# The first feed-forward's second product by seven products for eight, with its weight sums made in DRAM beside its first product

## The chip, the cores and the metric

One core of one Trainium2 chip runs the whole program. The metric is device time in microseconds of one execution, the median of several. A run's profile covers one execution of its own.

## The reference

Two layers over 512 tokens of width 1024. Each layer is a gated feed-forward (ffn1), a token mixer with three kinds of attention, and a second gated feed-forward (ffn2), each followed by a residual and a layer norm. All of it is float32. What the change touches is the second matrix of the first feed-forward of layer 0.

```python
def _swiglu(x, w1, w2):
    gt, up = jnp.split(x @ w1, 2, axis=-1)
    return (jax.nn.silu(gt) * up) @ w2          # w1: 1024 x 5632, w2: 2816 x 1024

for l in range(DEPTH):                          # DEPTH = 2
    x = _layer_norm(DN_ALPHA * x + 0.5 * _swiglu(x, ffn1_w1[l], ffn1_w2[l]), ln1_g[l], ln1_b[l])
    mix = _token_mix(x, w_in[l], ...)
    x = _layer_norm(DN_ALPHA * x + mix, ln2_g[l], ln2_b[l])
    x = _layer_norm(DN_ALPHA * x + 0.5 * _swiglu(x, ffn2_w1[l], ffn2_w2[l]), ln3_g[l], ln3_b[l])
```

## The kernel before

**Arithmetic.** Every float32 operand is split into a high part (ScalarE copies it to fp32r) and a low part (VectorE subtracts), and a product of two operands is three matmuls: high by high, low by high, high by low. `wsplit` (L155 ScalarE, L156 VectorE) does that for weights, `parts` (L483) for activations.

**A feed-forward** (`ffn`) has two products on TensorE, one after the other. The first makes the hidden rows, 22 blocks `f` of 128. The blocks 0 to 3 are plain; from block 4 on, `seven` loads the block's gate columns (`rg`, L422) and up columns (`ru`, L423), makes sums of them on VectorE (`ws`, L429 to L432), splits them, and `strassen` does seven products for eight, 84 matmuls with 256 columns. In it ScalarE copies the first two products out of PSUM (`sn`, L525), and TensorE's sixth product, which writes the same bank again, waits for that copy. `evac` (`t`, L473, then L474) writes the finished hidden block into `ha` or `hb`.

The second product contracts the 22 chunks of the hidden rows with w2. There are two forms of it. `rows_ln` is plain: for each chunk 4 token blocks by 2 column halves by 3, 24 matmuls of 128x512. `strassen_rows` takes the first 18 chunks as 9 pairs, each pair by seven products for eight, which is 42 matmuls for 48, and the last 4 chunks (`NTAIL`) plain. It needs four sums of the pair's blocks of w2, called t1 to t4. They do not depend on any activation.

**The weight sums.** `weight_sums` puts a queue of steps into `sums`; each step is one DMA from GpSimd's queue (L397) of 128x3x512 float32, 768 KB, from DRAM to DRAM, for three pairs at once. A step either copies a block of w2 into `ts` or adds a block to what stands there. `sums_step` issues the next step: a one-column copy on GpSimd first waits for a tile that some engine has just written, and so paces the steps. In the kernel before, the steps run in the mixer, for the two feed-forwards that come behind it. The first feed-forward of layer 0 has no mixer ahead of it, gets `ts = None`, and so takes `rows_ln`.

**Order.** TensorE and GpSimd run in the order of the code. VectorE, ScalarE and SyncE's DMA queue run in the order that a scheduler chose from its own estimate of times when the program was built; on the chip each of them keeps that order. Tiles come from rings of buffers: the raw weight columns `raw` have three. In the built program the gate columns of block f+1 go, from block 6 on, into the buffer that held the gate columns of block f.

**Side traffic.** In the first product of layer 0, `seven` also issues one table broadcast per block from GpSimd (`bvec`, L435 and L436), 16 in all, behind the block's `ws`.

Of the kernel before, what the change touches and what calls it, by code (L numbers as in the profile page):

```python
# [9 lines left out]
F32 = mybir.dt.float32  # L10
F32R = mybir.dt.float32r
BF = mybir.dt.bfloat16
AF = mybir.ActivationFunctionType
OP = mybir.AluOpType
# [50 lines left out]
def body(tc, a, out, depth=DEPTH):  # L65
# [199 lines left out]

    def strassen_rows(w2, ts, sp, plain, ln, clear, nxt, tmp):


        def acc8():
            return [ps(name="acc") for _ in range(8)]  # L270
# [12 lines left out]
        for p in range(NS):  # L283
            if p == 2:
                extra.pool = rp
            rb, ra = wraw(), wraw()
            nc.sync.dma_start(flat(rb)[:, 0:512], w2[2 * p * P:(2 * p + 1) * P, 0:512])
            nc.sync.dma_start(flat(rb)[:, 512:1024], ts[:, p, 1024:1536])
            nc.sync.dma_start(flat(ra), ts[:, p, 0:1024])
            sh, sl = sp(p)  # L290
            ub, ua = wsplit(rb), wsplit(ra)
            prods = [(0, 0, ub, lo4), (1, 3, ub, hi4), (2, 1, ua, hi4), (3, 2, ua, lo4)]
            for i, j, w, c in prods[:1] + prods[2:] + prods[1:2] if p == 0 else prods:
                for b in range(2):
                    mm(a1[2 * i + b], (sh[:, j], sl[:, j]), w, b, c, p == 0, p == NS - 1)
# [34 lines left out]
        for p in range(NS):  # L330
            uc, d, dc = weights(p)
            sh, sl = sp(p, True)
            prods = [(0, 1, uc, lo4), (1, 0, uc, hi4), (2, 2, d, dc)]
            for i, j, w, c in prods[2:] + prods[:2] if p == NS - 1 else prods:
                for b in range(2):
                    mm(a2[2 * i + b], (sh[:, j], sl[:, j]), w, b, c, p == 0, False)
            if p in (1, 2):
                merge(p - 1)
        rest = []
        for k in range(2 * NS, KF):  # L340
            rest.append((k, plain(k), wrows(w2, k)))
        extra.pool.release()
        extra.pool = None
# [34 lines left out]
        return pts  # L378

    NTAIL = 4  # L380
    NS = 9
    NG = 3
    sums = deque()

    def weight_sums(w2):


        ts = dram.tile([P, NS, 2048], F32, name="ts", tag="ts", bufs=3)
        n = NS // NG

        def step(g, i):
            c = slice(n * g, n * g + n)
            v = w2[2 * n * g * P:2 * n * (g + 1) * P].rearrange("(q two p) f -> two p q f", two=2, p=P)
            b11, b12, b21, b22 = (v[j][:, :, 512 * k:512 * k + 512] for j in range(2) for k in range(2))
            t1, t3, t2, t4 = (ts[:, c, 512 * k:512 * k + 512] for k in range(4))
            o, x = ((t1, b11), (t3, b12), (t2, b22), (t1, b12), (t4, b21), (t3, b22), (t2, t1), (t4, t2))[i]
            nc.gpsimd.dma_start(o, x, **({"accum_op": OP.add} if i in (3, 5, 6, 7) else {}))  # L397

        for g in range(NG):
            sums.extend(lambda g=g, i=i: step(g, i) for i in range(8))  # L400
        return ts

    def sums_step(t, psum=False):
# [59 lines left out]
    def ffn(l, w1, w2, which, xap, xa, wts, pend, done_prev, last, nxt, ts):  # L463
# [9 lines left out]
            nc.scalar.activation(t, pg, AF.Silu)  # L473
            nc.vector.tensor_tensor(hpart(f), t, pu, op=OP.mult)  # L474

        made, hs = {}, {}

        def h_parts(k, t):
            parts(t[:, 0], t[:, 1], hpart(k))
            hs[k] = t  # L480

        def parts(hi, lo, x):
            nc.scalar.activation(hi, x, AF.Copy)  # L483
            nc.vector.tensor_tensor(lo, x, hi.bitcast(F32), op=OP.subtract)
# [67 lines left out]
        evac(0, pts[0], pts[1])  # L552
        evac(1, pts[2], pts[3])
        for f in range(2, KF):
            if f == KF - 1 and ts is None:
                for k, n in enumerate(("hi", "lo")):
                    h_parts(k, wt.tile([P, KD, P], F32R, name=n, tag=n, bufs=3)
                            .rearrange("p (a b) c -> p a (b c)", a=2))
            elif f == KF - 1:
                w = [wt.tile([P, KD, P], F32R, name=n, tag=n, bufs=3).rearrange("p (a b) c -> p a (b c)", a=4)  # L560
                     for n in ("hi", "lo")]
                v, sn = (st.w1p.tile([P, 2, 256], F32, name=n, tag=n, bufs=2) for n in ("v", "sn"))
                made[0] = s_parts(0, w, v, sn[:, 0])
# [14 lines left out]
        for tb in range(NB):  # L578
            nc.gpsimd.dma_start(xa[tb], x_sp[tb * P:(tb + 1) * P, :])
        hsp = pool("hsp", side="right", reuse_waits="tile")  # L580
        ln = LN(hsp, which, l, xa, 0.5, last, ts is not None)

        def wload(k):
            if k not in hs:
                h_parts(k, hsp.tile([P, 2, S], F32R, name="hs", tag="hs", bufs=6))
            return wrows(w2, k)

        def pair():
            return [hsp.tile([P, 4, 256], F32R, name=n, tag=n, bufs=4) for n in ("sh", "sl")]
# [20 lines left out]
            r = [ln.row(n) for n in "GB"]  # L610
            return [[t[:, 0:S] for t in v]] + [[t[:, 0:S], t[:, S:D]] for t in r]

        if ts is None:
            wts, pend = rows_ln(KF, wload, lambda k: hs[k][:, 0], lambda k: hs[k][:, 1], ln, NA, fa.release, nxt)
        else:
            wts, pend = strassen_rows(w2, ts, sp, plain, ln, fa.release, nxt, tmp)

        def done():
            nx_close()
# [903 lines left out]
        tables(*tabs)  # L1523
        init.release()
    wts = pre
    ts = [None]
    for l in range(depth):
        fin = l == depth - 1
        wts, pend, done, xap, xa = ffn(l, a["ffn1_w1"][l], a["ffn1_w2"][l], 0, xap, xa, wts, pend, done, False,
                                       lambda: mix_first(l), ts.pop(0))  # L1530
        ts += [weight_sums(w) for w in [a["ffn2_w2"][l]] + ([] if fin else [a["ffn1_w2"][l + 1]])]
        wts, pend, done, xap, xa = mix(l, wts, pend, done, xap, xa, lambda: ffn_first(a["ffn2_w1"][l]))
        assert not sums
        wts, pend, done, xap, xa = ffn(l, a["ffn2_w1"][l], a["ffn2_w2"][l], 2, xap, xa, wts, pend, done, fin,
# [31 lines left out]
```

## Time and profile before

| what | us |
|---|---|
| median of 3 runs (2469.45 to 2471.69) | 2469.77 |
| the profiled execution: its own time | 2472.68 |
| the profiled execution: its span | 2470.9 |
| TensorE busy, of the span | 2443.8 (99%) |
| VectorE busy | 1763.6 (71%) |
| ScalarE busy | 1171.5 (47%) |
| GpSimd busy | 328.0 (13%) |

The granted TensorE clock is 0.997 over the span. In the profile's rows PE is a matmul, PEld a weight load, DVE VectorE, ACT ScalarE, POOL GpSimd, and SPq SyncE's DMA queue. A row of the timeline begins with the start and the duration in us. Matmuls overlap in the pipeline, so the rate at which they go is the distance from one start to the next, not the duration of one. A DMA row's duration is that of the issue; the time to its landing stands in the view of its line.

### The profile page before, as it was taken

Reading aid. Unit: us, or ns where it says so; the run is one execution under the profiler, and the core shown is the slowest. Engines: PE = TensorE matmul, PEld = TensorE weight load, DVE = VectorE, ACT = ScalarE, POOL = GpSimd, SP = SyncE. Lnnn points to the kernel's source line nnn. Section 1 sums busy time; section 2 is a strip of 40 time slices with the busy share of each in tenths; the row PEclk is TensorE's granted clock in tenths of the full one; section 3 lists DMA queues with packets and bytes.
Section 4 is the critical chain, followed back from the end, with each engine's and each line's share of the span. In section 5 each row is a group of like instructions: output and inputs, shape, how many; then the busy total and the mean of one; then the engine's idle time right before and its main releaser. Section 6 shows DMA issues by size and latency. Waiting matters only on the chain. (4 is left out here: it accounts for less than half of the span.)

```text
span 2470.9 us, 41023 instructions
## 1 busy us (share of the span) xinstructions
PE 2443.8 (99%) x15529; PEld 2157.1 (87%) x15529; DVE 1763.6 (71%) x3554; ACT 1171.5 (47%) x2262; POOL 328.0 (13%) x598
## 2 busy tenths in 40 slices
PE   9999999999999999999999999999999999999998
PEld 8999888788888789999889998877888888899987
DVE  7888355687653367988879889756776543698887
ACT  4444334576632343445534446445766422344463
POOL 2000000144432210000000000001444100000000
PEclk9999999999999999999999999999999999999999
DMA  7345434656579952336633346646655833323463
GB/s 207 104 120 143 140 96 127 183 152 146 127 209 237 251 172 82 103 104 210 203 98 99 104 144 211 186 113 168 157 155 114 227 102 122 112 87 109 131 210 127
DMA packets 411462, 364.07 MB, mean 147 GB/s; under 512 B 19720, under 2 KB 351640, under 8 KB 411264
## 3 DMA queue, kind: packets, MB, share of 16 engines
q1 hardware_dynamic: 381968, 279.92, 38.5%
q0 software_dynamic: 29296, 81.53, 13.2%
q8 instruction: 122, 2.00, 0.3%
q14 instruction: 76, 0.62, 0.1%
HBM read 334.07 MB, written 74.51 MB: 165 GB/s over the span
## 5 line engine op out<-in xcount | busy, mean ns | idle before, releaser
L156 DVE TENSOR_TENSOR lo<-raw,hi 128x1024 fp32r<-128x1024 f32 (+2 forms) x384 | 450.5, 1182 | 384.4 <-ACT hi L155 380.0
L155 ACT ACTIVATE hi<-raw 128x1024 fp32r<-128x1024 f32 (+2 forms) x384 | 390.1, 1023 | 598.5 <-DMA raw<-in_ffn_w_dram 136.3
L176 PE MATMUL pj<-xh,hi 128*128 128x512 f32 (+1 forms) x720 | 267.0, 371 | 0.1
L177 PE MATMUL pj<-xl,hi 128*128 128x512 f32 (+1 forms) x720 | 254.7, 354 | 1.1 <-DVE xl L242 1.1
L178 PE MATMUL pj<-xh,lo 128*128 128x512 f32 (+1 forms) x720 | 254.7, 354 | 0.0
L518 PE MATMUL pg<-xh,hi 128*128 128x256 f32 x864 | 245.0, 284 | 1.6 <-ACT sn L525 1.6
L518 PE MATMUL pg<-xh,lo 128*128 128x256 f32 x864 | 244.5, 283 | 0.0
L518 PE MATMUL pg<-xl,hi 128*128 128x256 f32 x864 | 244.5, 283 | 0.0
L438 ACT ACTIVATE hi<-ws 128x1024 fp32r<-128x1024 f32 x144 | 151.2, 1055 | 159.7 <-DVE ws L430 69.9
L439 DVE TENSOR_TENSOR lo<-ws,hi 128x1024 fp32r<-128x1024 f32 x144 | 175.4, 1221 | 17.8 <-ACT hi L438 17.7
L275 PE MATMUL acc<-hi,sh 128*128 128x512 f32 x450 | 175.4, 390 | 0.0
L275 PE MATMUL acc<-lo,sh 128*128 128x512 f32 x450 | 175.1, 389 | 0.0
L275 PE MATMUL acc<-hi,sl 128*128 128x512 f32 x450 | 175.1, 389 | 0.0
L518 PEld LDWEIGHTS pg<-xh,hi 128*128 128x128 f32 x864 | 165.8, 192 | 2.7 <-ACT sn L525 2.5
L518 PEld LDWEIGHTS pg<-xl,hi 128*128 128x128 f32 x864 | 165.8, 192 | 0.2
L518 PEld LDWEIGHTS pg<-xh,lo 128*128 128x128 f32 x864 | 165.8, 192 | 0.0
L518 PE MATMUL pu<-th,hi 128*128 128x256 f32 x576 | 163.0, 283 | 0.0
L518 PE MATMUL pu<-tl,hi 128*128 128x256 f32 x576 | 163.0, 283 | 0.0
L518 PE MATMUL pu<-th,lo 128*128 128x256 f32 x576 | 163.0, 283 | 0.0
L178 PEld LDWEIGHTS pj<-xh,lo 128*128 128x128 f32 x720 | 136.3, 189 | 19.6
L176 PEld LDWEIGHTS pj<-xh,hi 128*128 128x128 f32 x720 | 136.7, 190 | 15.3 <-issue 3.1
L177 PEld LDWEIGHTS pj<-xl,hi 128*128 128x128 f32 x720 | 137.0, 190 | 13.0 <-DVE xl L242 1.6
(368 smaller groups left out, 6259.9 us busy)
## 6 DMA issues: line engine op xcount, KB each, us to landing
raw<-in_ffn_w_dram SPq DMA_DIRECT2D x237, 512.0 KB, 4.0
ts<-in_ffn_w_dram POOLq DMA_DIRECT2D x54, 768.0 KB, 9.1
raw<-in_w_in_dram SPq DMA_DIRECT2D x56, 512.0 KB, 4.1
raw<-in_w_gate_dram SPq DMA_DIRECT2D x48, 512.0 KB, 5.2
raw<-ts SPq DMA_DIRECT2D x39, 512.0 KB, 4.2
ts<-ts POOLq DMA_DIRECT2D x18, 768.0 KB, 9.5
x_sp<-xa POOLq DMA_DIRECT2D x24, 512.0 KB, 6.1
ks<-hl SPq DMA_DIRECT2D x96, 128.0 KB, 2.4
```

What stands on the lines that cost most here:

```text
L155: nc.scalar.activation(hi[:, c], raw[:, c], AF.Copy)
L156: nc.vector.tensor_tensor(lo[:, c], raw[:, c], hi[:, c].bitcast(F32), op=OP.subtract)
L176: nc.tensor.matmul(o, hi[:, k], vh, start=first, stop=False)
L177: nc.tensor.matmul(o, hi[:, k], vl, start=False, stop=False)
L178: nc.tensor.matmul(o, lo[:, k], vh, start=False, stop=last)
L275: nc.tensor.matmul(o, xx[:, t], ww[:, c], start=first and i == 0, stop=last and i == 2)
L438: nc.scalar.activation(hi, x, AF.Copy)
L439: tt(lo, x, hi.bitcast(F32), op=OP.subtract)
L518: nc.tensor.matmul(o, wx, vx, start=first and k == 0 and i == 0, stop=k == 3 and i == 2, skip_group_check=True)
```

## The change

The first feed-forward of layer 0 gets weight sums for 6 pairs (chunks 0 to 11) and takes `strassen_rows` too. Chunks 12 to 17 are done plainly in the same accumulators, chunks 18 to 21 as before. Its 16 steps (two groups of three pairs, eight steps each) are issued as follows: twelve in the first product, at blocks 4 to 20 except each third, each paced by the hidden block before; four beside the pairs 0 to 3 of the second product, paced by the pair's split hidden rows. The order of the steps changes for all feed-forwards: t1, t3, t2 copied and then added to, for all groups, and t4 (a copy and an add) of all groups at the end. `rows_ln` stays in use for the mixer's output alone.

```diff
 def strassen_rows(w2, ts, sp, plain, ln, clear, nxt, tmp):
+        NS = ts.shape[1]
...
             sh, sl = sp(p)
+            sums_step(sh[:, 0].bitcast(F32))
             ub, ua = wsplit(rb), wsplit(ra)
...
+        for k in range(2 * NS, KF - NTAIL):
+            x, w = plain(k), wrows(w2, k)
+            for tb in range(NB):
+                for hf in range(2):
+                    mm(accs[tb][hf], x, w, tb, slice(4 * hf, 4 * hf + 4), tb >= 2 and hf == 1 and k == 2 * NS, False)
         rest = []
-        for k in range(2 * NS, KF):
+        for k in range(KF - NTAIL, KF):
...
-    def weight_sums(w2):
+    def weight_sums(w2, ns):
...
-            o, x = ((t1, b11), (t3, b12), (t2, b22), (t1, b12), (t4, b21), (t3, b22), (t2, t1), (t4, t2))[i]
-            nc.gpsimd.dma_start(o, x, **({"accum_op": OP.add} if i in (3, 5, 6, 7) else {}))
-
-        for g in range(NG):
-            sums.extend(lambda g=g, i=i: step(g, i) for i in range(8))
+            o, x = ((t1, b11), (t3, b12), (t2, b22), (t1, b12), (t3, b22), (t2, t1), (t4, b21), (t4, t2))[i]
+            nc.gpsimd.dma_start(o, x, **({"accum_op": OP.add} if i in (3, 4, 5, 7) else {}))
+
+        for r in (range(6), range(6, 8)):
+            for g in range(ns // n):
+                sums.extend(lambda g=g, i=i: step(g, i) for i in r)
...
         for f in range(2, KF):
-            if f == KF - 1 and ts is None:
...
+            if f >= 4 and f % 3:
+                sums_step(hpart(f - 1))
...
-    ts = [None]
+    ts = [weight_sums(a["ffn1_w2"][0], 6)]
...
-        ts += [weight_sums(w) for w in [a["ffn2_w2"][l]] + ([] if fin else [a["ffn1_w2"][l + 1]])]
+        ts += [weight_sums(w, 9) for w in [a["ffn2_w2"][l]] + ([] if fin else [a["ffn1_w2"][l + 1]])]
```

The scheduler made another order of the first product too. Three places of it are shown. The numbers in the names are the program's own: in the kernel before, `raw_1891`, `raw_2144` and `raw_2269` belong to the blocks 14, 16 and 17, and `pg_1919` and `pg_2045` to the blocks 14 and 15; in the kernel after, `raw_1908`/`raw_1909`, `raw_2034`/`raw_2035` and `raw_2162` are the blocks 14, 15 and 16, and `pg_1936` and `pg_2062` the blocks 14 and 15.

ScalarE around the copy `sn` of block 15, before:

```order
L155 ACTIVATE hi_2273<-raw_2269 128x1024
L473 ACTIVATE t_2014<-pg_1919 128x512
L525 ACTIVATE sn_2072<-pg_2045 128x512
L438 ACTIVATE hi_2279<-ws_2284 128x1024
L440 ACTIVATE dh_2155<-raw_2144 128x512
L438 ACTIVATE hi_2277<-ws_2283 128x1024
```

and after:

```order
L155 ACTIVATE hi_2166<-raw_2162 128x1024
L444 ACTIVATE hi_2042<-ws_2048 128x1024
L446 ACTIVATE dh_2046<-raw_2035 128x512
L444 ACTIVATE hi_2044<-ws_2049 128x1024
L479 ACTIVATE t_2031<-pg_1936 128x512
L527 ACTIVATE sn_2089<-pg_2062 128x512
```

Ahead of `sn` of block 15 stood the split of the gate columns of block 17, two blocks on; now the last such split ahead of it is that of block 16, one block on.

VectorE at the sums of block 14, before (`raw_1892` are the up columns of block 14, `pu_1668` belongs to block 12):

```order
L156 TENSOR_TENSOR lo_1896<-raw_1891,hi_1895 128x1024
L474 TENSOR_TENSOR ha_473<-t_1636,ha_473 128x512
L429 TENSOR_TENSOR ws_1905<-raw_1892 128x512
L431 TENSOR_TENSOR ws_1906<-raw_1891,raw_1892 128x512
L430 TENSOR_TENSOR ws_1905<-ws_1905,raw_1891 128x512
L432 TENSOR_TENSOR ws_1906<-raw_1891,ws_1905 128x512
L529 TENSOR_TENSOR v_1720<-pu_1668,sn_1694 128x256
L530 TENSOR_TENSOR v_1720<-pu_1668,v_1720 128x256
```

and after (`pu_1809` belongs to block 13):

```order
L156 TENSOR_TENSOR lo_1913<-raw_1908,hi_1912 128x1024
L435 TENSOR_TENSOR ws_1922<-raw_1909 128x512
L447 TENSOR_TENSOR dl_1793<-raw_1781,dh_1792 128x512
L539 TENSOR_TENSOR pg_1680<-pg_1680,v_1733 128x256
L436 TENSOR_TENSOR ws_1922<-ws_1922,raw_1908 128x512
L480 TENSOR_TENSOR ha_474<-t_1775,ha_474 128x512
L445 TENSOR_TENSOR lo_1917<-ws_1922,hi_1916 128x1024
L531 TENSOR_TENSOR v_1861<-pu_1809,sn_1835 128x256
L437 TENSOR_TENSOR ws_1923<-raw_1908,raw_1909 128x512
L438 TENSOR_TENSOR ws_1923<-raw_1908,ws_1922 128x512
```

The sums of block 14 stood among the results of block 12 and now stand among those of block 13, and the first sum, which reads the up columns, stands ahead of the finish of block 12 (L539). The buffers of `raw` now rotate over all three: the gate columns of block f+1 go where the up columns of block f-1 were, and the up columns of block f+1 where the gate columns of block f were.

GpSimd at the blocks 9 to 11, before:

```order
L435 COPY pace_88<-ws_1276 128x1
L436 DMA bvec_93<-bsml_92 128x1x384
L435 COPY pace_88<-ws_1402 128x1
L436 DMA bvec_93<-bsml_92 128x1x384
L435 COPY pace_88<-ws_1528 128x1
L436 DMA bvec_93<-bsml_92 128x1x384
```

and after:

```order
L441 COPY pace_88<-ws_1285 128x1
L442 DMA bvec_93<-bsml_92 128x1x384
L414 COPY pace_88<-ha_474 64x1
L402 DMA ts_201<-in_ffn1_w2_dram 128x3x512
L441 COPY pace_88<-ws_1413 128x1
L442 DMA bvec_93<-bsml_92 128x1x384
L414 COPY pace_88<-ha_474 64x1
L402 DMA ts_201<-ts_201 128x3x512
L441 COPY pace_88<-ws_1541 128x1
L442 DMA bvec_93<-bsml_92 128x1x384
```

Two steps of the sums, both of them adding, have come in between, each behind a hidden block and each directly ahead of a table broadcast.

More of the change, by code (lines that the diff above doesn't have):

```diff
@@ L380, in body @@
     NTAIL = 4
-    NS = 9
-    NG = 3
     sums = deque()
-    def weight_sums(w2):
-        ts = dram.tile([P, NS, 2048], F32, name="ts", tag="ts", bufs=3)
-        n = NS // NG
+    def weight_sums(w2, ns):
+        ts = dram.tile([P, ns, 2048], F32, name="ts", tag=f"ts{ns}", bufs=3 if ns == 9 else 1)
+        n = 3
         def step(g, i):
@@ L474, in evac @@
             nc.vector.tensor_tensor(hpart(f), t, pu, op=OP.mult)
[L476 to L480, printed above, removed]
+        made = {}
         def parts(hi, lo, x):
@@ L554, in ffn @@
         for f in range(2, KF):
-            if f == KF - 1 and ts is None:
[L556 to L559, printed above, removed]
+            if f >= 4 and f % 3:
+                sums_step(hpart(f - 1))
+            if f == KF - 1:
                 w = [wt.tile([P, KD, P], F32R, name=n, tag=n, bufs=3).rearrange("p (a b) c -> p a (b c)", a=4)
@@ L580, in ffn @@
         hsp = pool("hsp", side="right", reuse_waits="tile")
[L581 to L586, printed above, removed]
+        ln = LN(hsp, which, l, xa, 0.5, last, True)
         def pair():
@@ L611, in tmp @@
             return [[t[:, 0:S] for t in v]] + [[t[:, 0:S], t[:, S:D]] for t in r]
[L613 to L616, printed above, removed]
+        wts, pend = strassen_rows(w2, ts, sp, plain, ln, fa.release, nxt, tmp)
         def done():
```

## The prediction

> **What bounds the kernel now.** I read the page's first part, then the stages, then single engines at the places where TensorE waits. The page first, busy time by engine:
>
> ```profile
> PE 2443.8 (99%) x15529; PEld 2157.1 (87%) x15529; DVE 1763.6 (71%) x3554; ACT 1171.5 (47%) x2262; POOL 328.0 (13%) x598
> ```
>
> TensorE is busy 99%, so the time is the number of matmuls times their spacing, plus few waits. The stages follow, cut at the first matmul of each: three first products (layer 0's ffn1 and ffn2, layer 1's ffn1), then the second products of the same three, then the two mixers. Columns: the stretch, its length, busy time of each engine with the instructions, granted clock, DMA share, GB/s.
>
> ```profile
> 40.37:248.07 207.70, 206.05 (x1609) 201.00 (x1609) 172.05 (x263) 87.86 (x113) 18.56 (x36) 0.99 0.44 120
> 938.68:1141.90 203.22, 203.22 (x1611) 199.46 (x1609) 180.15 (x273) 91.81 (x117) 1.60 (x3) 1.00 0.37 108
> 1278.40:1481.62 203.22, 203.22 (x1611) 199.45 (x1609) 180.93 (x274) 92.71 (x117) 1.60 (x3) 1.00 0.37 108
> 248.07:369.58 121.51, 121.51 (x546) 100.77 (x545) 57.50 (x80) 43.40 (x61) 2.76 (x7) 1.00 0.40 118
> 1141.90:1251.61 109.71, 109.70 (x493) 90.53 (x491) 96.64 (x136) 63.52 (x80) 2.75 (x7) 1.00 0.61 193
> 1481.62:1590.91 109.29, 109.29 (x492) 90.63 (x491) 97.91 (x141) 65.04 (x85) 2.75 (x7) 1.00 0.61 190
> 369.58:865.93 496.35, 490.14 (x2902) 402.85 (x2900) 286.46 (x902) 245.28 (x692) 148.30 (x253) 1.00 0.69 179
> 1590.91:2081.73 490.82, 487.36 (x2901) 402.09 (x2900) 292.64 (x908) 247.80 (x695) 116.19 (x206) 1.00 0.56 149
> ```
>
> The fourth row is the stage that the change rewrites, in its plain form. The fifth and sixth show the other form at work, with 9 pairs. How fast 128x512 matmuls follow each other stands in TensorE's timeline of the plain form; the first and last of 197 rows in a row:
>
> ```profile
> 279.83 0.39 PE L191 MATMUL acc<-lo,hs 128*128 128x512 f32 x1
> ...
> 324.26 0.39 PE L189 MATMUL acc<-hi,hs 128*128 128x512 f32 x1
> ```
>
> That is 44.43 us for 196 steps, 0.2267 us each.
>
> **The second product.** Each of the 6 pairs needs 42 matmuls for 48, so 36 go: 36 x 0.2267 = 8.2 us. Whether new waits give some back is answered by the two stages that have the form already: with 9 pairs there are 54 fewer, and 121.51 - 109.29 = 12.2 us is 0.226 us for each. The form costs TensorE nothing, although VectorE is busy 97.91 of 109.29 us there. So the splits of hidden rows, which are removed (22) and come back as sums of halves, the merges and the later loads of the norm's rows are costed at nothing; TensorE's matmuls cover them. If that cover went, VectorE's 11 us of slack would go first; with 6 pairs it has less to do per matmul. Term: **-8.2 us**.
>
> **The old waits in the first product.** Layer 0's first product takes 4.5 us more than the others. One part is the start of the stage, which stays. The other is four waits of TensorE for `sn`, by the waits of that stretch, of which one is shown with its causes, engine by engine (TensorE's row before and at the wait, ScalarE, SyncE's queue, VectorE, GpSimd):
>
> ```profile
> PE pg L518 <- ACT sn L525: 1.6, 4, 0.7
> ...
> 181.95 0.28 PE L518 MATMUL pv<-th,dl 128*128 128x256 f32 x1
> 182.88 0.39 PE L518 MATMUL pg<-xh,hi 128*128 128x256 f32 x1 [0.65 <-ACT sn L525]
> ...
> 180.80 1.06 ACT L155 ACTIVATE hi<-raw 128x1024 fp32r<-128x1024 f32 x1 [2.89 <-PE pu L518]
> 181.76 0.58 ACT L473 ACTIVATE t<-pg 128x512 f32<-128x512 f32 x1
> 182.24 0.59 ACT L525 ACTIVATE sn<-pg 128x512 f32<-128x512 f32 x1
> ...
> 175.34 0.37 SPq L422 DMA_DIRECT2D raw<-in_ffn_w_dram  x1
> 178.62 0.37 SPq L423 DMA_DIRECT2D raw<-in_ffn_w_dram  x1
> 186.33 0.37 SPq L422 DMA_DIRECT2D raw<-in_ffn_w_dram  x1
> ...
> 174.58 0.69 DVE L432 TENSOR_TENSOR ws<-raw,ws 128x512 f32<-128x512 f32 x1
> ...
> 174.53 0.52 POOL L436 DMA_DIRECT2D bvec<-bsml  x1
> ```
>
> Read backwards: `sn` stood in ScalarE's queue behind the split of the gate columns of block 17, two blocks on; those were asked for at 175.34, the moment that L432 (174.58 + 0.69) let their only buffer go, and 0.8 us behind a table broadcast. The wait's 0.65 us of idle shows as 0.93 from start to start against some 0.12, so four waits with 1.6 us idle are about 2.2 us. In the changed order the split ahead of `sn` is that of block 16, whose columns are wanted anyway within a block's time (10.1 us), and the gate columns no longer wait for L432 of the block before. Term: between -2.2 and 0; the cause is gone, so I take **-2.2 us**. If another load is late instead, it is the up columns, which now do wait for that instruction.
>
> **What the twelve new transfers cost the first product.** Nothing of them runs on TensorE. GpSimd's share is twelve copies and issues, of the size of the next fence's POOL row (1.24 us), beside 18.56 us busy in 207.70: free time covers it. The broadcasts queue behind them and so behind the hidden block before; the last leaves near 230 us, and the first reader, `tab` below, starts at 373.64. Not so the weight loads: they share the DMA engines. The nearest rows are two equal loads in the mixer, `nck`, 512 KB, each with an adding step nearby, and a weight load behind a copying step; the issues, and then the landing by the load's line:
>
> ```profile
> 528.02 1.24 POOL L397 DMA_DIRECT2D ts<-in_ffn_w_dram  x1
> 529.96 0.34 SPq L1212 DMA_DIRECT2D nck<-ncd  x1
> ...
> DMA to landing us min/median/max: 8.2/8.2/8.2
> ...
> 576.38 1.12 POOL L397 DMA_DIRECT2D ts<-ts  x1
> 576.79 0.34 SPq L1212 DMA_DIRECT2D nck<-ncd  x1
> ...
> DMA to landing us min/median/max: 4.5/4.5/4.5
> ...
> 612.49 0.77 POOL L397 DMA_DIRECT2D ts<-in_ffn_w_dram  x1
> 615.80 0.58 SPq L162 DMA_DIRECT2D raw<-in_w_gate_dram  x1
> ...
> DMA to landing us min/median/max: 6.1/6.1/6.1
> ...
> 373.64 0.37 SPq L689 DMA_DIRECT2D tab<-bvec  x1
> ```
>
> The `nck` issued 1.9 us behind an adding step lands 3.7 us later than the one issued 0.4 us behind. The weight load 3.3 us behind a copying step lands after 6.1 us; against the 4.3 of the next fence that is 1.8 us more. In the first product the step leaves after the hidden block (L480), and the next up columns leave after L438, which stands behind L480 by about three sums and a split: the worse of the two distances. The up columns' landings in layer 0's first product, and those of all steps in the first part of the mixer, are these (L423, then L397):
>
> ```profile
> L423 SPq DMA_DIRECT2D raw<-in_ffn_w_dram x11: 367/368/368, 115.0 to 221.6; - x11
> ...
> DMA to landing us min/median/max: 3.7/4.3/5.0
> ...
> L397 POOL DMA_DIRECT2D ts<-in_ffn_w_dram x12: 769/802/1268, 499.9 to 649.6; - x12
> L397 POOL DMA_DIRECT2D ts<-ts x4: 1120/1242/1260, 564.5 to 671.1; - x4
> ...
> DMA to landing us min/median/max: 4.7/7.0/10.1
> ```
>
> What stands against such a delay is VectorE's idle time, since VectorE waits for the up columns at L435 with the previous blocks' results behind it, which TensorE waits for. In the undisturbed first product VectorE idles 203.22 - 180.15 = 23.1 us over 20 blocks, 1.15 us each, or 19.6 us over the 17 blocks 4 to 20. Lower bound of the cost: 0, if all delays fit. Upper bound: six adding steps at 3.7 us and six copying steps at 1.8 are 33.0 us, and each has only its own block's idle time against it, 12 x 1.15 = 13.8: 19.2 us. I take a value near the lower end, because a copying step, landed after 4.7 us or a little more, is nearly done when the next up columns start (some 3 us behind it, and slow to begin themselves), and because the blocks without a step save idle time for those with one: six times 3.7 = 22.2 less 19.6 is 2.6 us. Neighbouring adding steps (blocks 10 and 11, 19 and 20) can't use the idle time of distant blocks; for them I add half of one step's remainder (3.7 - 1.15 = 2.6), 1.3 us. Term: **+4 us**, between 0 and +19.
>
> The Trainium skill, "DMA: Bandwidth & Descriptors", section "Issuing engines are not separate DMA queues", says that transfers of all issuing engines run on the same 16 DMA engines and interleave; the two `nck` rows agree, 8.2 against 4.5 us. By the fit in its section "Anatomy of one DMA — SWDGE (gpsimd) path" (2.0 us and 436 GB/s) I estimate 1.8 us of moving for 768 KB; were each of the twelve to delay a load by that, 21.6 less 19.6 would leave +2.0, and the sum would be 2 us lower. It has no term for adding, whose landings here reach 10.1.
>
> **Four steps beside the second product.** They and the pairs' loads meet between about 248 and 275 us. The loads of layer 0's ffn2 run far ahead there:
>
> ```profile
> 1133.60 0.33 SPq L287 DMA_DIRECT2D raw<-in_ffn_w_dram  x1
> ```
>
> This is the third pair's, used at 1141.90 + 48 x 0.2267 = 1152.8, 19 us on. A delay of 3.7 us is covered, unless several pile up. The fourth pair's load waits for the last step of block 20, issued near 232 us and landed by 242 at 10.1 us; that pair starts at 248 + 72 x 0.2267 = 264. Bounds 0 and +2; I take 0.
>
> **The other feed-forwards' sums.** Same number and size, another order. The mixer of layer 0, with 48 steps, takes 496.35 us, that of layer 1, with 24, takes 490.82, so crowding could matter there by at most the 5.5 us between; order alone I put between -2 and +2, and take 0.
>
> **Sum.** -8.2 - 2.2 + 4 = -6.4 us. The profiled execution took 2472.68 (its span 2470.9), 2.9 above the median of 2469.77; taken from it the sum gives 2466.3, and from the median **2463.4 us**, which is the forecast.
>
> **Rivals.**
> - *Slower: the sums crowd out the columns.* Place: VectorE at L435, for the up columns. Each of the twelve steps costs its full price and idle time can't be saved up. The order of VectorE speaks for it: the sums of a block now stand one block ahead of TensorE, not two, so a late load has less lead to use up. The decisive point is 15.3 us of new waits (8.2 + 2.2 + 4.9), or 1.3 us for each step. At the upper bound, with 1 us in the second product, it is -10.4 + 19.2 + 1: 2479.6. The Trainium skill's rule on interleaving, named above, points this way too.
> - *No change.* Each adding step still costs 1 to 2 us after the idle time, 6 to 12 us in place of 4: 2465.4 to 2471.4. For it speaks the price of 3.7 against 1.15 of idle, against it that the load's distance to the step isn't fixed.
> - *The transfers are hidden altogether.* The copies land early, the additions fit into the idle time: -10.4, or 2459.4. For it speaks that the gate columns gain a whole block's time.
> - *The change doesn't do what it says*: the second product becomes VectorE's. The sixth row above speaks against it, at 0.226 us for each matmul saved; I give it no share of its own.
>
> **How the numbers follow.** A measurement of this kernel can tell about 0.2%, 4.9 us. Forecast, 3 to 5.5 us of new waits: 0.40. Hidden altogether, 0 to 3: 0.20. No change: 0.28. Slower: 0.12. So faster 0.60, same 0.28, slower 0.12. The forecast's own range is 2462 to 2465 (2469.8 - 10.4 plus 3 to 5.5). The range from 2458 (hidden, with 1.4 of the mixer's 2) to 2472 leaves out most of the slower case and a little below.
>
> **What would show it.** The second product's stage at 113.3 us (121.51 - 8.2) with no waits of TensorE. In layer 0's first product: 207.70 less 2.2 plus 4, 209.5 us; no wait for `sn` behind a split of gate columns; VectorE's `ws` (L435) waiting for `raw`, in the blocks with adding steps above all, and TensorE's waits at the weights' low parts. Wrong would be a stage above 113.3 + 2, a first product above 214 us, or a mixer moved by more than 2 us.

## The result and the profile after

The kernel after takes 2486.68 us (median of 6 runs, 2482.20 to 2489.23), the kernel before 2469.61 in the runs beside it: a ratio of 1.0065, with a 95% interval of 1.0052 to 1.0078. It is slower by some 17 us where 6 us of gain were forecast. The profiled execution took 2487.1, its span 2485.1.

Busy time by engine, from the page of the kernel after:

```profile
PE 2443.0 (98%) x15493; PEld 2156.8 (87%) x15493; DVE 1795.3 (72%) x3604; ACT 1188.1 (48%) x2280; POOL 346.9 (14%) x630
```

TensorE has 36 matmuls fewer, as the change says, and is busy for almost the same time: 2443.0 after 2443.8. So the 36 have gone, but others take longer, and the span has grown by waits. Layer 0's first product, its second product and the mixer behind it, by stage (columns as in the prediction):

```profile
40.42:270.55 230.13, 213.99 (x1609) 206.94 (x1609) 167.96 (x261) 86.74 (x113) 31.70 (x59) 0.96 0.58 143
270.55:391.03 120.48, 116.14 (x510) 94.86 (x509) 90.87 (x132) 59.33 (x80) 9.50 (x16) 0.99 0.62 193
391.03:882.90 491.87, 487.82 (x2902) 402.19 (x2900) 290.94 (x906) 247.32 (x695) 147.58 (x254) 1.00 0.71 182
```

The first product goes from 207.70 to 230.13, the second from 121.51 to 120.48 only, the mixer from 496.35 to 491.87. Two columns of the first row belong together: 230.13 less 213.99 is 16.1 us without a matmul (1.65 before), and the same matmuls that were busy for 206.05 us are now busy for 213.99, at a granted clock of 0.96 for 0.99.

Who waits in the first product (waiter, what for, us, times, longest):

```profile
DVE ws L435 <- DMA raw<-in_ffn_w_dram: 38.2, 12, 6.0
PE pg L520 <- DVE lo L445: 5.6, 5, 1.6
PE pg L520 <- ACT sn L527: 4.9, 3, 2.3
PE pg L520 <- ACT hi L444: 4.4, 3, 3.9
```

VectorE's first sum of a block (L435, L429 before) waits for the up columns 12 times. TensorE then waits for the parts that come out of those sums, or for the copy `sn`, which stands on ScalarE behind their splits. The place is the one that the prediction named for its slower rival.

The longest of these waits can be followed engine by engine: GpSimd's queue, SyncE's queue, VectorE, ScalarE, TensorE (start, duration, and in brackets the idle time before and what ended it):

```profile
113.49 1.32 POOL L402 DMA_DIRECT2D ts<-in_ffn_w_dram  x1 [0.37 <-issue]
...
116.36 0.37 SPq L429 DMA_DIRECT2D raw<-in_ffn_w_dram  x1
...
126.57 0.69 DVE L435 TENSOR_TENSOR ws<-raw 128x512 f32<-128x512 f32 x1 [6.04 <-DMA raw<-in_ffn_w_dram]
...
129.10 2.01 ACT L444 ACTIVATE hi<-ws 128x1024 fp32r<-128x1024 f32 x2 [8.57 <-DVE ws L436]
...
126.06 0.28 PE L520 MATMUL pg<-xh,lo 128*128 128x256 f32 x1
130.21 0.58 PE L520 MATMUL pg<-th,hi 128*128 128x256 f32 x1 [3.88 <-ACT hi L444]
...
133.01 0.41 PE L520 MATMUL pg<-tl,hi 128*128 128x256 f32 x1
133.22 0.41 PE L520 MATMUL pg<-th,lo 128*128 128x256 f32 x1
```

An adding step leaves at 113.49. The up columns are asked for 2.9 us behind it, at 116.36, and VectorE gets them at 126.57, 10.2 us later. TensorE has nothing for 4.15 us from start to start. The last two rows show what no term of the prediction had: behind the wait the matmuls start 0.21 us apart, for 0.12 us ahead of it. By stretch (the column behind GpSimd's is the granted clock):

```profile
120.00:126.00 6.00, 6.00 (x52) 6.00 (x52) 0.54 (x1) 0.53 (x2) 0.00 (x0) 1.00 0.94 254
126.00:134.00 8.00, 3.36 (x15) 2.86 (x15) 7.36 (x12) 3.47 (x4) 0.00 (x0) 0.73 0.25 72
134.00:140.00 6.00, 6.00 (x43) 6.00 (x42) 5.36 (x9) 2.49 (x4) 2.00 (x4) 0.78 0.29 87
...
189.00:193.00 4.00, 2.38 (x20) 2.17 (x19) 4.00 (x7) 1.06 (x1) 1.05 (x2) 1.00 0.83 268
228.00:232.00 4.00, 4.00 (x36) 4.00 (x35) 0.39 (x1) 0.05 (x1) 0.00 (x0) 1.00 0.96 284
234.70:239.00 4.30, 4.26 (x23) 4.26 (x24) 4.30 (x7) 2.51 (x3) 0.00 (x0) 0.60 0.39 108
```

In the third stretch 43 matmuls go where 52 went in the first, with TensorE busy throughout. The other three stretches show that a shorter wait can do it too: one of 2.40 us (232.34 to 234.74) is followed by 4.3 us at a clock of 0.60, while one of 1.90 us (at 189.57) leaves the clock at 1.00. Three waits of the first product, of 4.15, 2.54 and 2.40 us, are followed by such a stretch. There 21, 17 and 17 matmuls are some 0.09 us late each, so a stretch costs 1.5 to 2.2 us, and the three together 5.1.

How long the up columns take to land, in the kernel after and in one with its order and its pace copies but no transfers (`e7_paces`, below); for each the issues of their line, and then the landing:

```profile
L429 SPq DMA_DIRECT2D raw<-in_ffn_w_dram x16: 367/368/368, 68.0 to 247.2; - x16
...
DMA to landing us min/median/max: 3.7/6.6/10.2
```

```profile
L429 SPq DMA_DIRECT2D raw<-in_ffn_w_dram x16: 367/368/368, 68.0 to 222.7; - x16
...
DMA to landing us min/median/max: 3.6/4.3/5.7
```

### The profile page after: what moved, and what is told of

It reads as the page before. It is cut to its first block, busy times and chain, and to the rows that moved or that the text cites. A ratio compares the mean times of both kernels' runs of the same rounds, so it can differ in the third digit from the quotient of the medians.

```text
span 2485.1 us, 41053 instructions
## 1 busy us (share of the span) xinstructions
PE 2443.0 (98%) x15493; PEld 2156.8 (87%) x15493; DVE 1795.3 (72%) x3604; ACT 1188.1 (48%) x2280; POOL 346.9 (14%) x630
## 4 chain that ended last, share of the span: by engine, by line
PE 87%; DMA 5%; DVE 4%; issue 2%; ACT 1%; POOL 0%; SPq 0%; DVEq 0%; POOLq 0%; ACTq 0%
PE acc L276 16%; PE pg L520 14%; PE pu L520 7%; PE pj L176 5%; PE pj L177 5%; PE pj L178 5%; PE pv L520 3%; PE gate L176 3%; PE gate L177 3%; PE gate L178 3%; DMA raw<-in_ffn_w_dram 3%; PE brp L177 2%; PE brp L178 2%; PE brp L176 2%; PE sN L1067 2%
## 5 line engine op out<-in xcount | busy, mean ns | idle before, releaser
L156 DVE TENSOR_TENSOR lo<-raw,hi 128x1024 fp32r<-128x1024 f32 (+2 forms) x393 | 461.4, 1183 | 314.5 <-ACT hi L155 313.1
L155 ACT ACTIVATE hi<-raw 128x1024 fp32r<-128x1024 f32 (+2 forms) x393 | 398.9, 1024 | 545.9 <-DMA raw<-in_ffn_w_dram 129.4
L276 PE MATMUL acc<-lo,sh 128*128 128x512 f32 x606 | 236.3, 390 | 2.1 <-DVE lo L156 2.1
L276 PE MATMUL acc<-hi,sh 128*128 128x512 f32 x606 | 236.5, 390 | 1.6 <-ACT hi L155 1.6
L276 PE MATMUL acc<-hi,sl 128*128 128x512 f32 x606 | 235.8, 389 | 0.0
```

The lines of the kernel that those rows point to most:

```text
L155: nc.scalar.activation(hi[:, c], raw[:, c], AF.Copy)
L156: nc.vector.tensor_tensor(lo[:, c], raw[:, c], hi[:, c].bitcast(F32), op=OP.subtract)
L276: nc.tensor.matmul(o, xx[:, t], ww[:, c], start=first and i == 0, stop=last and i == 2)
```

## The experiments

Two theories stood at the start. The *transfers* theory: the loads are late because the twelve transfers move beside them. The *queue* theory: what costs is the order that the change brought about, the sums one block ahead of TensorE instead of two, with the pace copies on GpSimd ahead of the broadcasts. All diffs are against the kernel after, unless they say otherwise, and the comparisons are with the kernel before.

**No steps.** Leaves out the sums of the first feed-forward: the second product reads rows of w2 in their place.

```diff
-    ts = [weight_sums(a["ffn1_w2"][0], 6)]
+    ts = [a["ffn1_w2"][0][0:1536].rearrange("(p q two) f -> p q (two f)", q=6, two=2)]
```

> The changed kernel without the 16 steps of the first feed-forward's sums and without their pacing copies; the loads of the sums read plain rows of w2 of the same size instead, so those values are left out of the result. Its built program has the order of the first product that the kernel before has. Theory 'transfers' (the steps' traffic makes the weight columns late) and theory 'queue' (GpSimd's copies ahead of the table broadcast hold up VectorE's sums, and the order loses one block of lead) expect the same here: first product of layer 0 at 207.7 us as before, second product at 113.3 us, and with the mixer's 4 to 6 us a time of 2455 to 2458. A third theory, that the pairs' form itself waits in layer 0, expects the second product to stay near 120 us and the time near 2463.

Measured: 2455.73 us, ratio 0.9952 (0.9937 to 0.9967). The first two stages:

```profile
39.05:245.52 206.47, 205.95 (x1610) 200.89 (x1609) 173.09 (x267) 88.09 (x115) 28.88 (x37) 0.99 0.44 122
245.52:358.89 113.37, 113.37 (x511) 94.04 (x509) 87.42 (x126) 58.15 (x78) 2.76 (x7) 1.00 0.51 162
```

The second product takes 113.37 us with no idle time, where the prediction had 113.3. So the steps, with the pace copies and the order that come with them, cost everything else. But without their pace copies the scheduler also kept the order of the kernel before (the split two blocks ahead), so this run alone doesn't part transfers from order.

**The order of the steps alone.** The kernel before, with only the new order of the steps (t4 of all groups last), for the feed-forwards that had sums already.

> The kernel before with one part of the change alone: the new order of the sums' steps for the three later feed-forwards. If the order makes what the changed kernel gains in the mixer of layer 0 and just behind it (496.35 to 491.87 us, and 37.28 to 35.36 us in its last product), this has the same, a mixer near 492 us and a time of 2461 to 2465. If that gain comes from what runs ahead of the mixer, the mixer stays at 496 us and the time at 2469.6.

Measured: 2462.38 us (9 runs, 2458.73 to 2463.70), ratio 0.9974 (0.9964 to 0.9984). The mixer, and the last product behind it of before and then of this kernel:

```profile
364.74:855.37 490.63, 487.28 (x2901) 402.07 (x2900) 290.06 (x905) 246.81 (x693) 149.72 (x254) 1.00 0.70 182
```

```profile
865.93:903.21 37.28, 35.94 (x157) 29.07 (x156) 20.22 (x29) 11.09 (x12) 1.98 (x3) 1.00 0.70 196
```

```profile
855.37:890.73 35.36, 35.36 (x157) 29.23 (x156) 18.94 (x26) 11.27 (x13) 0.94 (x3) 1.00 0.63 200
```

The mixer loses 5.7 us (496.35 to 490.63) and the last product 1.9. In the trace of before TensorE waited in the mixer, at 818.05 and 820.16, for the split of gate weights whose load had lasted 17.1 us, from 801.55 on; with the slow matmuls behind these waits (eight of them 0.42 us apart, 822.15 to 825.13) that is about 4 of the 5.7 us. The copies that read `ts`, by their line in before and in this kernel:

```profile
L397 POOL DMA_DIRECT2D ts<-ts x12: 1120/1230/1260, 564.5 to 867.6; - x12
```

```profile
L397 POOL DMA_DIRECT2D ts<-ts x12: 1209/1212/1251, 548.6 to 849.7; - x12
```

The last step left at 867.6, in the last product, and now leaves at 849.7, ahead of it. That the waits are gone is seen in the rows; which part of the reordering removed them was not tried apart. I had costed the reorder at 0, between -2 and +2. The interval of the whole kernel's ratio, some 4 to 9 us of gain, excludes that.

**The step behind the broadcast.** The steps stand behind the block's table broadcast on GpSimd. All transfers stay, and VectorE and ScalarE have the order of the kernel before in the first product.

```diff
+        if f % 3:                                    # in seven, behind the broadcast
+            sums_step(hpart(f - 1))
...
-            if f >= 4 and f % 3:
-                sums_step(hpart(f - 1))
```

> The whole change, but in the first product each step's pacing copy and transfer stand behind the block's table broadcast in GpSimd's queue, not ahead of it, still paced by the hidden block before. All bytes are as in the change; the built program has the order of the kernel before. Theory 'transfers': first product within 4 us of the changed kernel's 230, time 2480 to 2487. Theory 'queue': first product at 206 to 214 us, second product at 113 to 116, time 2456 to 2466.

Measured: 2494.28 us, ratio 1.0110 (1.0093 to 1.0126). The first product and two of its waits:

```profile
39.56:283.13 243.57, 217.78 (x1609) 211.71 (x1609) 171.95 (x268) 89.50 (x116) 42.50 (x60) 0.93 0.56 139
```

```profile
ACT hi L155 <- DMA raw<-in_ffn_w_dram: 61.5, 13, 8.0
...
PE pg L522 <- ACT sn L529: 25.8, 8, 5.6
```

With the old order back, it is 13 us worse than the kernel after. The gate columns are now the late ones, two blocks ahead of need, and ScalarE waits for them with `sn` of a nearer block behind. The order wasn't what cost; it decides who pays.

**Paces without transfers.** GpSimd's pace copies stay, the transfers go (the same part is left out as without steps).

```diff
-    sums = deque()
+    sums = deque([lambda: None] * 16)
...
-    ts = [weight_sums(a["ffn1_w2"][0], 6)]
+    ts = [a["ffn1_w2"][0][0:1536].rearrange("(p q two) f -> p q (two f)", q=6, two=2)]
```

> As the run without steps, but with the 16 pacing copies on GpSimd in their places; they release no transfer. The built program has the changed kernel's order (the split ahead of sn is that of the next block). Theory 'transfers': as without steps, within 2 us in each stage. Theory 'queue': the first product of layer 0 stays 8 to 20 us above 207.7, with VectorE's ws waiting for raw or for GpSimd's pace, and the time is 8 to 20 us above the run without steps.

Measured: 2453.78 us, ratio 0.9943 (0.9928 to 0.9958).

```profile
40.44:245.68 205.24, 205.24 (x1610) 200.96 (x1610) 171.39 (x267) 89.04 (x114) 20.36 (x48) 0.99 0.41 121
245.68:359.04 113.36, 113.36 (x511) 94.01 (x509) 87.43 (x126) 58.27 (x78) 4.88 (x11) 1.00 0.52 165
```

This has the order of the kernel after, with the split ahead of `sn` one block on, and TensorE has no idle time in either product. VectorE's wait for the up columns, 38.2 us in the kernel after, is here

```profile
DVE ws L435 <- DMA raw<-in_ffn_w_dram: 7.9, 9, 1.6
```

The queue theory falls. Measured against it, the transfers cost 24.9 us in the first product (230.13 - 205.24), of which 16.1 are idle time and 8.8 longer busy time (213.99 - 205.24), and 7.1 in the second (120.48 - 113.36), of which 4.3 are idle time and 2.8 longer busy time. Not all of the longer busy time is a lower clock. Taken from start to start in the trace of the kernel after, the twelve waits of the first product cost 18.1 us beyond the usual spacing, and the matmul behind each some 0.1 more; that makes 19.4, and the three slow stretches add 5.1.

**Copies only.** All sixteen transfers stay, none of them adds (so the sums are not made).

```diff
-            nc.gpsimd.dma_start(o, x, **({"accum_op": OP.add} if i in (3, 4, 5, 7) else {}))
+            nc.gpsimd.dma_start(o, x, **({"accum_op": OP.add} if i in (3, 4, 5, 7) and ns == 9 else {}))
```

> The whole change, but all 16 steps of the first feed-forward copy and none adds, so its sums are left out of the result; same number of transfers and bytes written, same order in the built program. If adding is what costs (3.7 us for an adding step against 1.8 for a copying one, as the prediction had it), the first product falls from 230 by 6 x 1.9 = 11 us to about 219 and the time to about 2475. If a copying step costs as much as an adding one, the first product stays within 4 us of 230.

Measured: 2470.66 us (10 runs), ratio 0.9998 (0.9989 to 1.0007).

```profile
39.15:257.40 218.25, 208.92 (x1609) 202.61 (x1609) 169.89 (x265) 88.16 (x114) 30.21 (x60) 0.99 0.55 154
```

Twelve copying steps cost 218.25 - 205.24 = 13.0 us, 1.1 each. Turning six of them into adding ones costs the remaining 11.9 us, 2.0 each; an adding step costs 3.1. The prediction had taken copying steps to be nearly free. The DMA shares of the three rows fit: share times length is 84 us without transfers (0.41 x 205.24), 120 with copies and 133 in the kernel after. By this estimate, from rounded shares, a copying step keeps the DMA engines busy for 3.0 us and an adding one for 2.2 us more.

**Later issue of the transfers.** The pace by the hidden block stays as a bare copy, and the transfer was meant to leave with the next up columns, by a second pace behind the last weight sum.

```diff
-                sums_step(hpart(f - 1))
+                nc.gpsimd.tensor_copy(pace[0:64], hpart(f - 1)[0:64, 0:1])
...
+        if f % 3:                                    # in seven, behind the broadcast
+            sums_step(x2[:, 4])
```

> The whole change with its pacing copies where they were (the built program keeps one block of lead), but each of the twelve transfers of the first product leaves GpSimd behind the table broadcast and a second copy, of the last weight sum of the next block. That sum (L438) also frees the buffer of the next up columns, so load and transfer start together instead of the transfer 2 to 3 us ahead. Theory 'distance' (a load loses by standing behind a transfer): first product at 206 to 214 us against the changed kernel's 230, time 2456 to 2468. Theory 'bytes' (the transfers take DMA time from the loads wherever they stand): first product at 224 to 234, time 2480 to 2490.

Measured: 2484.33 us, ratio 1.0058 (1.0042 to 1.0073).

```profile
38.86:271.86 233.00, 215.38 (x1610) 208.44 (x1609) 171.49 (x267) 88.69 (x115) 38.41 (x72) 0.95 0.58 146
```

It missed its aim: in eight blocks the transfer left 1.4 to 1.6 us ahead of the up columns, in three more 2.7 to 3.7 us, where it leaves 2.3 to 4.5 us ahead in the kernel after. That about half of the distance in most blocks changed little (233.00 for 230.13) is all that it says.

**The transfer at the time of the loads.** The same question with the single pace behind the last weight sum, in the order of the kernel before, so that it compares with the step behind the broadcast.

```diff
+        if f % 3:                                    # in seven, behind the broadcast
+            sums_step(x2[:, 4])
...
-            if f >= 4 and f % 3:
-                sums_step(hpart(f - 1))
```

> The kernel after with each of the twelve steps paced by the last weight sum of its block, so that it leaves at the same moment as the next block's loads, about 3 us later than behind the hidden block; VectorE's and ScalarE's order in the first product is that of the kernel before (split two blocks ahead), as in the kernel with the step behind the table broadcast. Bytes theory (some load meets each transfer wherever it leaves): first product 235 to 248 us, total 2485 to 2500. Distance theory (the load loses because the transfer has a start of some 3 us on it): first product below 218 us, total below 2472.

Measured: 2488.41 us, ratio 1.0072 (1.0058 to 1.0086).

```profile
39.01:276.53 237.52, 214.08 (x1610) 207.04 (x1609) 173.63 (x267) 87.02 (x114) 34.42 (x61) 0.96 0.56 144
```

Leaving with the loads instead of ahead of them saves 6 of 38 us (237.52 for 243.57, against 205.24 without transfers). The distance theory's forecast, below 218, fails, and the time lies where the other theory had it. But the aim was met for one load only: the transfer now leaves 0.6 us behind the gate columns and still 2.6 us ahead of the up columns, which take 6.0 us to land (median) and up to 9.0; without steps, in the same order, they take 3.8 and up to 4.8. So some load met the transfer wherever it was put; what the distance alone does to one load isn't shown.

**Four steps alone.** The first twelve steps are empty, the four beside the second product stay (the sums of the twelve are left out).

> As the run with paces alone (twelve steps that release nothing), but the four steps beside the second product are real transfers; the sums that the first twelve would make are plain rows of w2, and left out of the result. If the changed kernel's 7 us of waits in the second product come from these four, it stays at 118 to 121 us here. If they come from the late last steps of the first product, it is at 113.4 to 115.

Measured: 2461.03 us, ratio 0.9955 (0.9941 to 0.9969).

```profile
245.55:361.08 115.53, 114.49 (x510) 93.69 (x509) 87.60 (x126) 57.58 (x78) 12.06 (x15) 1.00 0.64 189
```

The stage lies between the two ranges expected. The four steps cost 2.2 us (115.53 - 113.36), just above the prediction's bound of 2. For the other 5 of the 7.1 us TensorE's waits in the second product of the kernel after say where they lie:

```profile
PE acc L276 <- ACT hi L155: 1.6, 1, 1.6
...
PE acc L276 <- DVE v L532: 1.4, 1, 1.4
...
PE acc L276 <- ACT t L479: 0.9, 1, 0.9
```

The last two are for results of the first product's last blocks (L532, L479), which VectorE and ScalarE finish late, and which hold the banks that `acc` needs; they stand at the stage's start, and a stretch of slow matmuls follows them (0.43 us apart from 276.6 to 279.6). From start to start that is 4.4 us. The first, at 315.57, is for the split of a plain weight load (L167) that left right behind the load of t4 (L325, at 309.62), which itself left when the last addition had landed; it belongs to the four steps. So the lateness of the first product is carried into the second. This is read from the trace; no run took it away alone.

**Three pairs.** Half of the change, six steps in every third block.

```diff
-            if f >= 4 and f % 3:
+            if f >= 4 and f % 3 == 1:
...
-    ts = [weight_sums(a["ffn1_w2"][0], 6)]
+    ts = [weight_sums(a["ffn1_w2"][0], 3)]
```

> The first feed-forward's second product by seven for eight for three pairs only: six steps beside the first product (three copying, then three adding), one in every third block, and two beside the second product. Price theory (each step costs its net price, 1.1 us copying and 3.1 adding, wherever it stands): first product 205.2 + 3 x 1.1 + 3 x 3.1 = 217.8 us, second product 117.4 to 119, total 2470 to 2474. Saving theory (VectorE's idle time of the two blocks without a step is used as well, 3.45 us for a step against 2.25 gross copying and 4.25 adding): first product 205.2 + 3 x 0.8 = 207.6 us, total 2459 to 2462.

Measured: 2483.87 us, ratio 1.0052 (1.0039 to 1.0065).

```profile
40.58:258.37 217.79, 208.90 (x1609) 202.71 (x1609) 170.80 (x266) 87.98 (x114) 22.41 (x47) 0.98 0.50 132
258.37:387.11 128.74, 122.74 (x528) 99.28 (x527) 78.47 (x113) 51.46 (x71) 5.56 (x12) 0.96 0.49 149
```

The first product is 217.79 us, at the 217.8 of the price theory: two blocks without a step between two steps spare nothing here, so idle time isn't saved up. The total was missed by 10 us all the same, in the second product (128.74, expected 117.4 to 119). GpSimd, SyncE's queue and TensorE there:

```profile
269.31 1.02 POOL L402 DMA_DIRECT2D ts<-ts  x1 [7.34 <-DMA ts<-in_ffn_w_dram]
...
279.06 0.80 SPq L325 DMA_DIRECT2D raw<-ts  x2
279.97 1.35 SPq L167 DMA_DIRECT2D raw<-in_ffn_w_dram  x3
...
277.97 0.39 PE L276 MATMUL acc<-lo,sh 128*128 128x512 f32 x1
282.36 0.52 PE L276 MATMUL acc<-hi,sh 128*128 128x512 f32 x1 [4.01 <-ACT hi L155]
```

With three pairs TensorE is through the products ahead of those with t4 at 277.97, 20 us into the stage. The addition to t4 left at 269.31; its reader (L325) left at 279.06, the moment it had landed, with three plain weight loads (L167) right behind it in SyncE's queue. TensorE waited 4.0 us, and once more for 1.8.

**Small transfers.** The same sums in pieces of 256 KB, one pair each: two in every block, three at each of the first pairs.

```diff
+            if q is not None:                        # q: the pair of the three
+                o, x = o[:, q:q + 1], x[:, q:q + 1]
...
-            if f >= 4 and f % 3:
+            if f >= 4:
                 sums_step(hpart(f - 1))
...
+        sums_step(x2[:, 4])                          # in seven, behind the last sum
```

> The same sums in transfers of a third of the size (128x1x512, 256 KB), two in every block from 4 on, one behind the hidden block and one behind the block's last weight sum; bytes as before. Bytes theory (a load loses in proportion to what moves beside it, and each block's idle time of 1.15 us is used): gross 24.9 + 12 x 1.15 = 38.7 us less 18 x 1.15 = 20.7 leaves 18, first product about 223 us, total 2472 to 2482. Price-by-transfer theory (each transfer costs much the same whatever its size): 36 of them, first product above 240 us, total above 2490. Burst theory (only a long transfer delays a load beyond the idle time of its block): first product below 212 us, total below 2465.

Measured: 2472.16 us (10 runs), ratio 1.0003 (0.9994 to 1.0013).

```profile
40.58:259.65 219.07, 209.98 (x1609) 202.77 (x1609) 172.94 (x267) 88.33 (x114) 52.67 (x110) 0.99 0.64 150
259.65:379.05 119.40, 116.79 (x510) 96.01 (x509) 88.07 (x127) 58.19 (x78) 16.79 (x30) 0.97 0.63 194
```

The first product falls from 230.13 to 219.07. The price for each transfer falls, the bytes theory (223) is nearest, and the burst theory (below 212) is out: the same bytes in thirds cost 13.8 us instead of 24.9. The run changed two things, though: the size, and the spread, since the thirds stand in every block from 4 on and the large steps in twelve of them. By the bytes theory's own sum the spread alone is worth 6.9 of the 11.1 us (6 x 1.15); what is left for the size was not tried apart. The DMA engines are busy for longer than in the kernel after (0.64 x 219.07 = 140 us against 133), so their total busy time is not what sets the price. The whole is no faster than the kernel before: 13.8 + 6.0 us for a gain of 8.2.

**Order and empty paces.** The kernel before with the new order of the steps, and with GpSimd's pace copies in the first product but nothing issued, so that the scheduler puts VectorE's sums one block ahead.

> The kernel before with the new order of the later feed-forwards' steps and with the twelve pacing copies in layer 0's first product, which release nothing; its second product stays plain. The order of the first product becomes that of the changed kernel. If the paces take away the waits for sn as they did in the run with paces alone (first product 205.24 us), the time is 0 to 2 us below that of the new order alone (2462.4): 2460 to 2462. Else it is the same within 1 us, or above.

Measured: 2460.51 us (2459.14 to 2463.88), ratio 0.9958 (0.9945 to 0.9970).

```profile
38.95:242.46 203.51, 203.51 (x1610) 199.60 (x1609) 169.68 (x263) 88.65 (x114) 20.57 (x49) 1.00 0.42 119
```

The first product has no idle time left. Of the 4.2 us between 207.70 and 203.51 some 1.7 lie at the stage's start, where the first matmuls were slow before (view in the next section) and are at full speed in this execution; this is not the paces' doing. This kernel keeps the plain second product and computes all of the reference; it beats both kernels, although its interval overlaps that of the step order alone (0.9964 to 0.9984).

## Why the prediction was wrong

Term by term, us; "measured" is a stage of the kernel named against the stage it stands beside.

| term | forecast | measured |
|---|---|---|
| 36 matmuls fewer in the second product | -8.2 | -8.15 (121.51 to 113.36, paces without transfers) |
| old waits for `sn` | -2.2 | -2.5 (207.70 to 205.24, the same) |
| twelve transfers beside the first product | +4, 0 to 19.2 | +24.9: 16.1 idle, 8.8 longer busy time |
| four steps beside the second | 0, to +2 | +7.1; alone +2.2 |
| the other feed-forwards' step order | 0, -2 to +2 | -6.4 (mixer 496.35 to 491.87, last product 37.28 to 35.36) |
| sum | -6.4 | +14.9 (the spans differ by 14.2, the medians by 17.1) |

**The step that failed** is the size of the third term: "I take a value near the lower end, because a copying step ... is nearly done when the next up columns start ..., and because the blocks without a step save idle time for those with one". Both reasons were wrong. Copies alone cost 1.1 us each beyond what the blocks absorb, and with two free blocks to each step the price for a step stayed as it was. The idle time was each block's own, as the slower rival had it, and the waits of the first product, 16.1 us idle or 19.4 from start to start, came out near the upper bound given (19.2), by the second count just above it. That VectorE had it in every block of the old trace did not make it a store.

**What no bound held** is the slow matmuls behind waits: three stretches in the first product, 5.1 us together, and one in the second, 1.6. The bounds were of waits, one for one; here some waits are followed by 4 to 5 us at a lower granted clock. The old trace shows this twice: in the mixer, behind the waits at 818.05 and 820.16 (a clock of 0.79 from 818 to 826), which the prediction did not read, and at the start of the stage, which I left alone as "the start of the stage, which stays". That stretch in the trace of the kernel before:

```profile
41.00:44.50 3.50, 3.50 (x11) 2.77 (x10) 3.50 (x6) 1.62 (x3) 1.42 (x3) 0.59 0.11 29
```

TensorE is busy throughout, at a granted clock of 0.59.

**The rival that came** was the slower one, with its place (L435) and its reason (the full price for each step, no saving). Its time, 2479.6 at its upper bound, was still 7 us low, and came that near in part by luck: the first product cost 5.7 us more than it had (24.9 for 19.2), the second 6.1 more (7.1 for 1), and the order of the other feed-forwards' steps, which it did not count, gave 6.4 back. The Trainium skill, "DMA: Bandwidth & Descriptors", section "Issuing engines are not separate DMA queues", said what happens: transfers of all issuing engines share the same 16 DMA engines and interleave. The up columns' median landing of 6.6 against 4.3 us agrees; the prediction cited the rule and gave it 0.12.

**The four steps**: the cover named was loads that run far ahead. Alone the steps cost 2.2 us, at the bound given. The last addition of the twelve was to leave near 232 and left at 258.86, and VectorE and ScalarE came late out of the first product, so a part of that term's error stands in this one.

**Right were** the second product's 113.3 (113.37 and 113.36 measured), the removed cause of the `sn` waits, and VectorE not becoming the bound of the second product (87.43 of 113.36 us busy). The `sn` term has a caution: without steps and in the old order the first product took 206.47, so perhaps only 1.2 of the 2.5 us are the order's, and the rest lies between executions.

**The reorder** of the other feed-forwards' steps was sized by a guess of 2 us either way, although the prediction had the 5.5 us between the two mixers in hand as the room for it. All of that room was taken.

## What to carry to other kernels

In these runs, idle time on an engine that waits in each iteration was an allowance for that iteration alone: price an added transfer by what the next load loses less one iteration's slack, and multiply by the number of transfers. Before moving sums into DRAM transfers, compare both sides for one unit of work: a pair here saves 6 matmuls, 1.36 us, and its eight quarter-megabyte pieces cost (24.9 + 7.1) / 6 = 5.3 us beside loads that TensorE needs, or 3.3 in smaller transfers spread over all blocks. The one part of the change that paid, the order of steps that were there already, was worth trying by itself: it gives 0.26% without any new transfer.

## What the runs showed of the hardware

- A wait of TensorE can cost more than its length. In the kernel after, behind waits of 4.15, 2.54 and 2.40 us the matmuls start 0.21 us apart instead of 0.12, for some 4.5 us, at a granted clock of 0.60 to 0.78 by stretch; behind one of 1.90 us the clock stays at 1.00. The length of a wait doesn't settle it: with three pairs one of 2.26 us (from 91.20) is followed by a clock of 0.66 (93.5 to 98.5) and one of 2.40 us (from 247.47) by 1.00, and with the transfer at the time of the loads even one of 3.48 us (from 149.16) is followed by 1.00. The Trainium skill, "TensorE: Matmul & The Clock Gate", section "Part 1: The HAM clock gate (the "warmup" mystery)", states half clock after at least one idle window of about 3.4 us, and full clock again after about as long a busy one. The slow rate and its length agree roughly; that waits of 2.26 and 2.40 us were enough is below the page's figure, and the traces decide. What else decides whether the clock falls stays open.
- An accumulating transfer from DRAM to DRAM costs its neighbours more than a copying one of the same 768 KB: 3.1 us against 1.1 net for each step here.
- The same bytes in pieces of a third, spread over every block from 4 on instead of twelve of them, cost the first product about half (13.8 us against 24.9); the shares of size and spread are open.
- What stays open: what the distance from a transfer to a single load does (moving all twelve changed 6 us of 38), and what exactly in the new step order freed the mixer.
